# Sums of the down weights made inside the block products, and gate products placed behind later copies

## The chip, the cores and the metric

The kernel runs on one core of a Trainium2 chip. The metric is the time of one execution in microseconds on the device, and lower is better. A run is an execution of the whole kernel, and the times given are medians over runs.

## The reference

The reference is a two-layer encoder over 768 tokens, a sample of 512 and a prompt of 256, each going through the layers by itself, with a model width of 1024. Layer 0 mixes tokens with a bidirectional mLSTM, layer 1 with sliding-window attention. Both are followed by a feed-forward net with a gate and a convolution of width 3 along the tokens. All is float32.

```python
for l in range(DEPTH):                      # 2
    ...
    y = mlstm_mixer(...) if l == 0 else swa_mixer(...)   # both end in "@ w_out"
    x = x + g1 * y
    h = rmsnorm(x, norm_g[l, 1]) * (1 + sc2) + sh2
    x = x + g2 * conv_ffn(h, ffn_w_up[l], ffn_conv_w[l], ffn_conv_b[l], ffn_w_down[l])
return rmsnorm(x, final_g)

def conv_ffn(h, w_up, conv_w, conv_b, w_down):
    u = h @ w_up                            # 768 x 1024 @ 1024 x 5632
    u = depthwise_conv3(u, conv_w) + conv_b
    g, val = u[..., :2816], u[..., 2816:]
    return (silu(g) * val) @ w_down         # 768 x 2816 @ 2816 x 1024
```

The change concerns the feed-forward net, above all its down projection, and what runs during the projection (`out_proj`) that ends the mixer before it.

## The kernel before, in words

**Precision.** Every float32 operand of a matmul is split into a high and a low part: ScalarE (ACT) casts the high one (L263), VectorE (DVE) subtracts it for the low one (L264), and TensorE (PE) makes three matmuls, high by high, high by low, low by high. A weight tile of 128x1024 float32 (512 KB) arrives by DMA in one of five `raw` buffers and is split into one of three `whi` and one of three `wlo` buffers.

**Up projection and gate.** The 2816 columns of the gate are 22 chunks of 128, taken two at a time as 11 parts (`up(p)`). A part needs two `pair` calls, one for the gate columns and one for the values. A pair is computed by a Strassen-Winograd scheme: seven block products, called quarters here, of 12 matmuls each, with the names B11, T1, T2, B21, T3, B22, T4. The sums of weights that this needs are made by POOL (GpSimd) from two loaded weight tiles (L1206, L1209, L1210, L1218); `wa`, `wb` and `wc` are the split weights. Sums of results are formed in PSUM: a "fork copy" on ACT copies a running sum from one bank to another (L1221 ahead of T2, L1234 after it), so that the quarter after it can add on top. Evictions (L1247, L1248 on DVE, L1186 and others on ACT) put the results in a row buffer. Then comes the convolution: ACT does the middle tap (L1484), DVE the outer two (L1486, L1487), and ACT the SiLU (L1494). 

**Gate product and operands.** Parts 2 to 9, eight parts, go through the blocked down projection. For such a part `operands` lets POOL multiply gate and values (L1511, four instructions) and DVE form the sums that the blocked scheme needs as right-hand operands (L1514 to L1517). The seven operands of a part are stored to DRAM (`yd`, L1521, issued by SP a pair later). Part 9's stay on the chip (`final`). Parts 0, 1 and 10 are multiplied by `product` (L1499) and projected directly by `down`.

**Blocked down projection.** `blocked` multiplies the down weights of the eight parts, as 2x2 blocks over their output columns and the parts' two chunks, with the operands in seven products of 96 matmuls each (Strassen-Winograd once more, 8 steps of k a product). A product's weights are four tiles of 512 KB, one for two steps of k. It accumulates in four X or four Y banks in PSUM; ACT copies banks to banks and DVE adds them to x (L593). Loads of weights are at L1303, loads of operands from `yd` at L1298; L383 loads x again, which had been saved to `xf`.

**Sums.** Four of the seven products need sums of the given weight blocks. `sums(l)` makes them ahead of time: it loads the 16 weight tiles of the eight parts, makes the sums on POOL (L1262, L1264, L1266, L1269; 32 instructions of 128x512 a layer) and stores them to DRAM as `sd` (16 stores). It is a generator, stepped three times after each tile of `out_proj` through `self.fills`. In layer 1 it also runs beside attention.

**Order.** A scheduler orders the instructions of each engine by its estimate of readiness and by program order. `issue_after` ties instructions behind a named one, and `manual_schedule` keeps the written order on the engines it lists. SP issues the loads and stores in the order of its queue and waits in it for buffers to come free.

Of the kernel before, what the change touches and what calls it, by code (L numbers as in the profile page):

```python
# [169 lines left out]
class Net:  # L170
    def __init__(self, tc, ctx, io):
        self.tc, self.nc, self.io = tc, tc.nc, io
        pool = lambda n, **k: ctx.enter_context(tc.tile_pool(name=n, bufs=1, **k))
        self.cp = pool("consts")
        self.hp = pool("acts")
        self.stg = pool("stage")
        self.big = pool("big")
        self.nt = pool("normtmp")
        self.psp = pool("psum", space=bass.MemoryType.PSUM)
        self.dp = pool("scratch", space=bass.MemoryType.DRAM)  # L180
        self.turn = 0
        self.n = 0
        self.fill = iter(())
        self.pend = []

        self.early, self.begun = {}, {}
        self.sd = {}
# [407 lines left out]
    def out_proj(self, u0, act, xt, l, apply):  # L595
# [26 lines left out]
        for i, (z, c, w) in enumerate(todo):  # L622
            if i in (KC, 2 * KC - 1):
                yield
            c0, c1, _ = HALVES[z]
            o = self.ps()[:, : c1 - c0]
            self.product(o, w, act, c0, c1, range(self.begun.pop(i, 0), KC))
            self.tick(4.2)
            for p0, p1, q in pieces(c0, c1):
                self.resid(xt, o[:, p0 - c0 : p1 - c0], l, 16, c, (p0, p1, q))  # L630
            norms[z].square(c)
            self.step(self.fills, 3)
            if i % KC == KC - 1:
                self.start(HALVES[z], norms[z].stages())
# [617 lines left out]
    def sums(self, l):  # L1252

        nc = self.nc
        tt = nc.gpsimd.tensor_tensor
        self.sd[l] = sd = self.dp.tile([NBLK, P, 2048], F32, name=f"sd{l}")
        for k in range(NBLK):
            u = U_FFN + (l * NPART + SOLO + k) * 3 + 2
            r = [self.load(u, h) for h in range(2)]
            s2, s4, s1, s3 = (t[:, 512 * i : 512 * (i + 1)] for t in r for i in range(2))  # L1260
            yield
            tt(s1, s1, s3, ALU.add)  # L1262
            yield
            tt(s2, s1, s2, ALU.subtract)  # L1264
            yield
            tt(s4, s4, s2, ALU.subtract)  # L1266
            nc.sync.dma_start(sd[k, :, :1024], r[0])
            yield
            tt(s3, s3, s2, ALU.subtract)  # L1269
            nc.sync.dma_start(sd[k, :, 1024:], r[1])  # L1270
            yield

    def blocked(self, l, xt, u, yd, xf):
# [3 lines left out]
        w, sd = self.io["w"], self.sd[l]  # L1277

        def given(i):
            return lambda k: w[u + 3 * k : u + 3 * k + 4 : 3, :, 512 * i : 512 * (i + 1)]  # L1280

        def summed(i):
            return lambda k: sd[k : k + 2, :, 512 * i : 512 * (i + 1)]
# [5 lines left out]
        parts = {}  # L1289

        def ready(i):
            if i >= len(stream):
                return
            src, z = stream[i]
            ys = self.slab([P, NBLK - 1, H])
            for k in K[::4]:
                e = min(k + 4, NBLK - 1)
                nc.sync.dma_start(ys[:, k:e], yd[k:e, :, z].rearrange("k p t -> p k t"))  # L1298
            ys = [ys[:, k] for k in K[:-1]] + [self.final[:, z]]
            for k in K:  # L1300
                if k % 2 == 0:
                    raw = self.stg.tile([P, 2, 512], F32, tag="raw", name=self.nm("raw"), bufs=5)
                    nc.sync.dma_start(raw, src(k).rearrange("k p c -> p k c"))  # L1303
                    wt = self.split(raw.rearrange("p k c -> p (k c)"))
                y = [self.tmp([P, H], R) for _ in range(2)]
                self.fp_copy_split(*y, ys[k])
                parts[i, k] = [t[:, 512 * (k % 2) : 512 * (k % 2 + 1)] for t in wt], y

        X = [self.pa()[:, :H] for _ in range(4)]
        Y = [self.bank[c][:, :H] for c in range(4)]  # L1310

        def add(c, c0, o):
# [6 lines left out]
            (X, late, True, lambda c: nc.scalar.copy(Y[c], X[c])),  # L1319
            (X, soon, False, lambda c: add(c, 0, X[c])),  # L1320
            (Y, late, False, lambda c: nc.scalar.copy(X[c], Y[c])),
            (Y, soon, False, lambda c: add(c, H, Y[c])),
            (X, late, False, lambda c: add(c + 4, H, X[c])),
            (Y, late, True, lambda c: (add(c, H, Y[c]), add(c + 4, H, Y[c]))),
            (X, late, False, lambda c: add(c + 4, 0, X[c])),
# [142 lines left out]
    def ffn(self, l, xt, pool, last_tile, apply, keep=None):  # L1468
# [10 lines left out]
        stores = []  # L1479
# [16 lines left out]
        def product(yrow, g):  # L1496
            for j in range(2):
                y = yrow[:, 2 + j]
                nc.gpsimd.tensor_tensor(y, y, yrow[:, j], ALU.mult)  # L1499
                self.fp_copy_split(g[:, 0, j], g[:, 1, j], y)  # L1500

        yd = self.dp.tile([NBLK - 1, P, 7, H], F32, name=f"yd{l}")

        def operands(yrow, k):
# [7 lines left out]
            b11, t3, b21, b22, t2, t4, t1 = (s[:, z] for z in range(7))  # L1512
            tt = nc.vector.tensor_tensor
            tt(t3, b22, t3, ALU.subtract)  # L1514
            tt(t2, b11, t3, ALU.add)
            tt(t4, b21, t2, ALU.subtract)
            tt(t1, b22, t2, ALU.subtract)  # L1517
            if k == NBLK - 1:
                self.final = s
                return  # L1520
            return lambda: nc.sync.dma_start(yd[k], s)  # L1521

        def up(p):
# [9 lines left out]
            for i in range(2):  # L1533
                if p:
                    rows = [urow[:, 2 * i + j] for j in range(2)]
                    with ExitStack() as order:
                        then = [held.pop()] if held else []
# [3 lines left out]
                        if i and stores:  # L1541
                            then.append(stores.pop())
# [5 lines left out]
                if i == 0:  # L1548
                    held.append(lambda: silu(yrow))
            if g is None:  # L1550
# [51 lines left out]

        prev = None
        for p in range(NPART):
            g = up(p)
            if prev is not None:
                down(*prev)
            if p == SOLO:
                xf = self.dp.tile([P, KC, T], F32, name=f"xf{l}")
# [3 lines left out]
        self.blocked(l, xt, u0 + 3 * SOLO + 2, yd, xf)  # L1613
# [20 lines left out]
    def block(self, l, act, xs):  # L1634

        with self.tc.tile_pool(name="ffn", bufs=1, reuse_waits="tile") as pool:
# [3 lines left out]
            self.fills = self.sums(l)  # L1640
# [156 lines left out]
```

## Time and profile before

| | |
|---|---|
| median of 3 runs | 1905.57 us (1902.56 to 1913.9) |
| profiled execution, its own time | 1909.98 us |
| its span, first to last instruction | 1908.2 us |
| mean granted TensorE clock | 0.970 |
| PE busy | 1793.6 us, 94% |
| DVE busy | 1378.4 us, 72% |
| ACT busy | 955.4 us, 50% |
| POOL busy | 602.6 us, 32% |
| moved by the main DMA queue | 279.90 MB |

Times in the table are microseconds. A share is busy time over the span and is an average over stages that have different limits. The bracket behind a row, such as `[1.55 <-ACT ps L1221]`, is how long the engine was idle just before that instruction and whose result ended the wait. A granted clock of 1.00 is full speed of TensorE.

### The profile page before, as it was taken

The page shows a single profiled execution, that of the slowest core. Times are in us where ns is not written, and L with a number is a line of the kernel's source. Part 1 is how long each engine was busy: PE and PEld are TensorE (multiplying, and loading weights), DVE is VectorE, ACT ScalarE, POOL GpSimd, SP SyncE. Part 2 cuts the span into 40 slices and gives each one's busy share as a digit, 9 for nine tenths or more (in the row PEclk, how much of TensorE's full clock was granted, in tenths as well). Part 3 has the DMA queues.
Part 4 walks back from the last instruction along what each step waited for, and adds up shares of the span by engine and source line. Part 5 has one row for each costly group of instructions (what it writes and reads, how often), then busy time and mean ns, then how long its engine had stood idle before and what let it go on. Part 6 is the DMA issues. An engine that isn't in the chain of part 4 may idle for free.

```text
span 1908.2 us, 29324 instructions
## 1 busy us (share of the span) xinstructions
PE 1793.6 (94%) x11098; PEld 1679.8 (88%) x11098; DVE 1378.4 (72%) x2077; ACT 955.4 (50%) x1935; POOL 602.6 (32%) x482
## 2 busy tenths in 40 slices
PE   6999999998799999999799999999999999997997
PEld 4988887988798999999799989889989989997997
DVE  4765677884589877787666767756898777877665
ACT  3444443442356445555454556654564455554543
POOL 2101001025514544655200203645134455542001
PEclk7999999999899999999899999999999999998999
DMA  8343566457822243232665321457222432336652
GB/s 323 114 157 120 177 211 214 153 172 245 296 72 79 89 140 125 95 124 97 220 202 178 123 78 51 153 165 262 81 79 77 150 125 96 114 105 193 218 168 67
DMA packets 111769, 281.77 MB, mean 148 GB/s; under 512 B 8631, under 2 KB 51127, under 8 KB 109836
## 3 DMA queue, kind: packets, MB, share of 16 engines
q1 hardware_dynamic: 111628, 279.90, 44.1%
q8 instruction: 87, 1.43, 0.3%
q14 instruction: 54, 0.44, 0.1%
HBM read 231.09 MB, written 48.77 MB: 147 GB/s over the span
## 4 chain that ended last, share of the span: by engine, by line
PE 44%; DVE 13%; POOL 5%; issue 5%; ACT 5%; DMA 4%; POOLq 0%; SPq 0%; DVEq 0%; ACTq 0%
PE pa L257 7%; PE ps L257 6%; PE ps L1173 6%; PE ps L1176 5%; PE ps L1174 5%; DMA raw<-in_w_dram 3%; DVE wlo L264 3%; PE pa L1338 2%; PE pa L1339 2%; PE pa L1337 2%; PE ps L1338 2%; PE ps L1337 2%; PE ps L1339 2%; ACT whi L263 2%; DVE slab L1486 2%
## 5 line engine op out<-in xcount | busy, mean ns | idle before, releaser
L264 DVE TENSOR_TENSOR wlo<-raw,whi 128x1024 fp32r<-128x1024 f32 x261 | 351.6, 1348 | 126.5 <-ACT whi L263 120.5
L263 ACT CAST whi<-raw 128x1024 fp32r<-128x1024 f32 x261 | 272.9, 1047 | 200.9 <-DMA raw<-in_w_dram 65.3
L1173 PE MATMUL ps<-zh,whi 128*128 128x384 f32 x504 | 172.7, 343 | 22.4 <-ACT ps L1221 22.0
L257 PE MATMUL ps<-zh,whi 128*128 128x256 f32 (+1 forms) x560 | 189.6, 340 | 2.5 <-ACT whi L263 1.9
L257 PE MATMUL ps<-zh,wlo 128*128 128x256 f32 (+1 forms) x560 | 185.1, 332 | 2.0 <-DVE wlo L264 2.0
L257 PE MATMUL ps<-zl,whi 128*128 128x256 f32 (+1 forms) x560 | 185.5, 333 | 0.0
L1176 PE MATMUL ps<-zh,wlo 128*128 128x384 f32 x504 | 171.7, 341 | 0.5 <-DVE wlo L264 0.4
L1174 PE MATMUL ps<-zl,whi 128*128 128x384 f32 x504 | 171.3, 340 | 0.8 <-DVE zl L1130 0.8
L257 PE MATMUL ps<-slab,whi 128*128 128x384 f32 x512 | 137.8, 351 | 14.6 <-ACT whi L263 14.1
L1484 ACT ACTIVATE slab<-slab,cstt 128x772 f32<-128x772 f32 x88 | 91.0, 1034 | 113.2 <-DVE slab L1247 112.2
L1486 DVE SCALAR_TENSOR_TENSOR slab<-slab,cstt,slab 128x771 f32<-128x771 f32 x88 | 114.7, 1305 | 35.4 <-ACT slab L1484 35.3
L257 PEld LDWEIGHTS ps<-zh,whi 128*128 128x128 f32 x560 | 107.8, 193 | 16.1 <-issue 4.4
L1173 PEld LDWEIGHTS ps<-zh,whi 128*128 128x128 f32 x504 | 95.6, 190 | 29.0 <-ACT ps L1221 26.8
L509 DVE SCALAR_TENSOR_TENSOR ada<-raw,silc,ada 128x1024 f32<-128x1024 f32 x84 | 110.2, 1349 | 14.8 <-DMA raw<-in_adaln_w_dram 14.8
L1206 POOL TENSOR_TENSOR raw<-raw 128x512 f32<-128x512 f32 x40 | 63.1, 1579 | 180.2 <-DMA raw<-in_w_dram 168.1
L1511 POOL TENSOR_TENSOR slab<-slab 128x512 f32<-128x512 f32 x64 | 97.5, 1544 | 66.7 <-DVE slab L1487 54.7
L257 PEld LDWEIGHTS ps<-zh,wlo 128*128 128x128 f32 x560 | 107.5, 192 | 12.4 <-DVE wlo L264 2.9
L257 PEld LDWEIGHTS ps<-zl,whi 128*128 128x128 f32 x560 | 107.6, 193 | 12.1 <-issue 3.4
L257 PEld LDWEIGHTS ps<-slab,whi 128*128 128x128 f32 x512 | 95.1, 195 | 18.6 <-ACT whi L263 17.3
L263 ACT CAST nt<-slab 128x384 fp32r<-128x384 f32 x112 | 56.8, 512 | 108.8 <-PE pa L1338 61.9
L1176 PE MATMUL ps<-yh,wlo 128*128 128x384 f32 x304 | 105.5, 347 | 4.7 <-DVE wlo L264 4.5
L264 DVE TENSOR_TENSOR nt<-slab,nt 128x384 fp32r<-128x384 f32 x112 | 60.7, 553 | 67.8 <-ACT nt L263 67.8
(316 smaller groups left out, 5175.9 us busy)
## 6 DMA issues: line engine op xcount, KB each, us to landing
raw<-in_w_dram SPq DMA_DIRECT2D x232, 512.0 KB, 4.1
raw<-in_adaln_w_dram SPq DMA_DIRECT2D x84, 512.0 KB, 4.5
yd<-slab SPq DMA_DIRECT2D x14, 1344.0 KB, 4.6
sd<-raw SPq DMA_DIRECT2D x32, 512.0 KB, 4.1
raw<-sd SPq DMA_DIRECT2D x32, 512.0 KB, 4.2
slab<-yd SPq DMA_DIRECT2D x14, 768.0 KB, 7.1
slab<-yd SPq DMA_DIRECT2D x14, 576.0 KB, 8.3
slab<-in_x_dram SPq DMA_DIRECT2D x12, 512.0 KB, 7.5
```

Of the source, the lines that this page charges most:

```text
L257: self.nc.tensor.matmul(out, lhsT, rhs, start=start, stop=stop)
L263: nc.scalar.copy(hi, src)
L264: return nc.vector.tensor_tensor(lo, src, hi.bitcast(F32), ALU.subtract)
L509: stt(acc[:, s], row, w, acc[:, s], ALU.mult, ALU.add)
L1173: mm(o, wh[:, k], hi[k], start=start and k == 0, stop=False, skip_group_check=True)
L1174: mm(o, wh[:, k], lo[k], start=False, stop=False, skip_group_check=True)
L1176: mm(o, wl[:, k], hi[k], start=False, stop=k == 3, skip_group_check=True)
L1337: mm(o[c], wh[:, cs], yh, start=start and k == 0, stop=False, skip_group_check=True)
L1338: mm(o[c], wh[:, cs], yl, start=False, stop=False, skip_group_check=True)
L1484: nc.scalar.activation(y, u, AF.Identity, bias=cb, scale=w(1))
L1486: stt(y[:, 1:], u[:, :-1], w(0), y[:, 1:], ALU.mult, ALU.add)
L1511: nc.gpsimd.tensor_tensor(row[:, p0:p1], yrow[:, 2 + j, b], yrow[:, j, b], ALU.mult)
```

## The change

The DRAM pass is gone: `sums`, `self.fills` and `self.sd` are removed. `blocked` makes the sums when it needs them. Its seven products come in a new order, with S1T1 (operand 6, weights a21 + a22) first. The columns of `stream` are the operand's index z, the two weight blocks, the engine and operation of the sum, and the index under which the sum is kept in DRAM for a later product. Kept sums are stored from POOL's own DMA queue.

```diff
-        stream = [
-            (given(0), 0), (given(1), 2), (summed(0), 4), (summed(1), 3), (summed(3), 1), (summed(2), 6), (given(3), 5),
-        ]
+        stream = [
+            (6, a21, a22, gp, ALU.add, 0),
+            (0, a11, None, None, None, None),
+            (2, a12, None, None, None, None),
+            (4, saved(0), a11, gp, ALU.subtract, 1),
+            (1, a11, a21, tt, ALU.subtract, None),
+            (3, a12, saved(1), tt, ALU.subtract, None),
+            (5, a22, None, None, None, None),
+        ]
...
+            z, a, b, op, how, keep = stream[i]
             for k in K:
                 if k % 2 == 0:
-                    raw = self.stg.tile([P, 2, 512], F32, tag="raw", name=self.nm("raw"), bufs=5)
-                    nc.sync.dma_start(raw, src(k).rearrange("k p c -> p k c"))
-                    wt = self.split(raw.rearrange("p k c -> p (k c)"))
+                    r = raw(a(k))
+                    if b:
+                        op(r, r, raw(b(k)), how)
+                    if keep is not None:
+                        nc.gpsimd.dma_start(sd[keep][k // 2], r)
+                    wt = self.split(r)
```

Per layer the weights of the products take 44 loads of 512 KB in place of 28, and 8 stores; the pass with its 16 loads and 16 stores falls away. The sums are 8 POOL and 8 DVE instructions of 128x1024 in place of 32 POOL instructions of 128x512. The results go to banks and to x in an order that fits (the first product is added to two rows of x at once, so the reload of x is needed by its end):

```diff
-            (X, late, True, lambda c: nc.scalar.copy(Y[c], X[c])),
-            (X, soon, False, lambda c: add(c, 0, X[c])),
...
+            (X, late, True, lambda c: (add(c, H, X[c]), add(c + 4, H, X[c]))),
+            (Y, late, True, lambda c: nc.scalar.copy(X[c], Y[c])),
+            (Y, soon, False, lambda c: add(c, 0, Y[c])),
+            (X, late, False, lambda c: nc.scalar.copy(Y[c], X[c])),
+            (Y, soon, False, lambda c: add(c + 4, H, Y[c])),
+            (X, late, False, lambda c: add(c, H, X[c])),
+            (Y, late, False, lambda c: add(c + 4, 0, Y[c])),
```

Second, `operands` is called behind a fork copy of the next part's second pair, and its DVE combinations behind one of the pair after that; the store follows them. `yd` becomes three DRAM tiles, of the first 4, the next 2 and the last part.

```diff
-            return lambda: nc.sync.dma_start(yd[k], s)
+            def combine():
+                b11, t3, b21, b22, t2, t4, t1 = (s[:, z] for z in range(7))
+                tt = nc.vector.tensor_tensor
+                tt(t3, b22, t3, ALU.subtract)
+                tt(t2, b11, t3, ALU.add)
+                tt(t1, b22, t2, ALU.subtract)
+                tt(t4, b21, t2, ALU.subtract)
+                if k < NBLK - 1:
+                    nc.sync.dma_start(yd[k // 2 - 1][k % 2] if k > 3 else yd[0][k], s)
+                else:
+                    self.final = s
+            later[SOLO + k + 2, 0] = combine
...
             if g is None:
-                stores.extend(filter(None, [operands(yrow, p - SOLO)]))
+                later[p + 1, 1] = lambda: operands(yrow, p - SOLO)
```

Third, `blocked` becomes a generator (`tail`) that asks for the operands of the first two products earlier, six parts of them at the start of part 10 and the seventh after its first pair; later products' operands are asked for two products ahead in place of one.

```diff
+        fetch(0, (0, 1))
+        fetch(1, (0, 1))
+        yield
+        fetch(0, (2,))
+        fetch(1, (2,))
+        yield
...
+        ready(0)
+        xt[:] = self.load_x(xf)
         for i, (o, order, start, done) in enumerate(steps):
-            for j in (0, 1) if i == 0 else (i + 1,):
-                ready(j)
-            if i == 0:
-                xt[:] = self.load_x(xf)
+            ready(i + 1)
+            fetch(i + 2)
```

In the changed file the lines shift: POOL's sums in `pair` are L1204, L1207, L1208, L1216, the fork copies L1219 and L1232, the weight loads L1289, the sums in `blocked` L1300, their stores L1302, the products L1510, the combinations L1515 to L1518, the block matmuls L1342 to L1344.

More of the change, by code (lines that the diff above doesn't have):

```diff
@@ L1250, in pair @@
         self.evict(r2, d)
[L1252 to L1271, printed above, removed]
@@ L1478, in ffn @@
         behind = []
-        stores = []
+        later = {}
         def conv(u, y, ch):
@@ L1536, in up @@
                     with ExitStack() as order:
[L1537 removed]
+                        then = [f for f in (held.pop() if held else None, later.pop((p, i), None)) if f]
                         for ins in behind[2 * i :] if p == 1 else ():
                             order.enter_context(self.tc.issue_after(ins))
[L1541 to L1542 removed]
                         other = p == i == 1
```

74 lines of the change are left out of this document (37 added, 37 removed).

## The prediction

> **What bounds the kernel now.** I read the page first, then TensorE's idle time in order of place, then the windows around each place.
>
> ```profile
> core 0: 1908.2 us, clock 0.970
> PE 1793.6 (94%) x11098; PEld 1679.8 (88%) x11098; DVE 1378.4 (72%) x2077; ACT 955.4 (50%) x1935; POOL 602.6 (32%) x482
> L1173 PE MATMUL ps<-zh,whi 128*128 128x384 f32 x504 | 172.7, 343 | 22.4 <-ACT ps L1221 22.0
> ```
>
> TensorE is the bound: busy for 1793.6 of 1908.2 us, so 114.6 us are idle. The change leaves the matmuls as they are. It can only win idle time back, and the little that TensorE loses by a lower clock after an idle stretch. The third row names one lump already: 22.0 us in which the first matmul of a quarter waits for the fork copy L1221. I take the four places that the change touches one by one. In the windows below the columns are stretch, length, busy time (and count) of PE, PEld, DVE, ACT, POOL, then granted clock, DMA share, GB/s.
>
> **1. The sums leave layer 0's output projection.** Removed, per layer, are 16 loads and 16 stores of 512 KB and 32 POOL adds of 128x512 that ran during `out_proj`.
>
> ```profile
> 440.00:460.00 20.00, 16.30 (x88) 15.16 (x87) 11.84 (x14) 5.34 (x9) 12.95 (x9) 0.94 0.92 317
> 460.00:480.00 20.00, 18.40 (x101) 17.76 (x101) 11.21 (x13) 4.52 (x6) 13.88 (x9) 0.98 0.78 280
> 480.00:500.00 20.00, 17.73 (x106) 17.00 (x104) 8.54 (x13) 6.50 (x9) 7.91 (x7) 0.96 0.93 316
> 500.00:520.00 20.00, 13.55 (x56) 11.76 (x56) 9.69 (x21) 7.01 (x15) 15.04 (x11) 0.78 0.82 287
> 520.00:540.00 20.00, 18.30 (x103) 18.30 (x103) 18.09 (x27) 12.66 (x26) 1.80 (x3) 0.91 0.56 186
> ```
>
> And what waits for what in 430 to 545, with its transfers:
>
> ```profile
> ACT whi L263 <- DMA raw<-in_w_dram: 28.3, 7, 9.4
> SPq L272 <- DMA sd<-raw: 21.4, 12, 4.1
> DMA packets 8844, 28.03 MB, mean 244 GB/s; under 512 B 864, under 2 KB 2400, under 8 KB 8837
> ```
>
> The five windows add up to 84.3 busy us of 100: 15.7 idle. The slow stretch costs more: 56 matmuls in 13.55 us are 0.242 each, against 18.30/103 = 0.178 in the next window, 56 x 0.064 = 3.6 us. The last three rows say what is late: the copy that starts a weight split waits 28.3 us for weights, and SP, which issues every load, is held 21.4 us by buffers still being stored to `sd`. Of the 28.03 MB, 32 transfers of 0.524 MB, 16.8 MB, are the sums'. Without them 11.2 MB are left for the same stretch and SP's queue holds loads alone. At most 15.7 + 3.6 = 19.3 us come back, about 21 if the edges of the stretch gain too; I keep two for the first weights and the norm at its end: **-17** (-10 to -21; the low end is half of the idle time and the slow matmuls).
>
> **2. The same in layer 1**, where the sums also ran beside attention.
>
> ```profile
> sum 150.00, PE 143.12 PEld 133.88 DVE 104.86 ACT 81.98 POOL 74.28; mean PE 47.71 PEld 44.63 DVE 34.95 ACT 27.33 POOL 24.76
> ```
>
> The wait itself:
>
> ```profile
> PE pa L1012 <- POOL t L1004: 2.2, 1, 2.2
> ```
>
> From 1210 to 1360 PE is idle for 6.9 us only; one wait of 2.2 is for a POOL step of attention that stands behind the adds. **-4** (-2, that wait alone, to -7, all of it).
>
> **3. Combinations behind the copies in the up projection.** The four POOL products (L1511) move behind the fork copy of the next part's second pair; the four DVE combinations (L1514 to L1517) get a place of their own after them; the `yd` store follows at once. Windows of six consecutive parts:
>
> ```profile
> 723.90:756.10 32.20, 30.66 (x176) 30.30 (x175) 25.06 (x24) 18.86 (x32) 17.14 (x12) 1.00 0.30 107
> 756.10:787.90 31.80, 29.82 (x170) 29.35 (x168) 25.36 (x25) 16.89 (x30) 18.89 (x12) 1.00 0.32 110
> 787.90:821.10 33.20, 31.59 (x170) 30.95 (x170) 25.61 (x25) 19.05 (x32) 17.75 (x12) 0.95 0.31 105
> 821.10:852.80 31.70, 29.72 (x170) 29.25 (x168) 25.26 (x25) 16.80 (x30) 18.68 (x12) 1.00 0.31 109
> 852.80:886.10 33.30, 31.69 (x170) 31.05 (x170) 25.71 (x25) 19.19 (x32) 17.57 (x12) 0.95 0.32 107
> 886.10:916.10 30.00, 29.61 (x169) 29.28 (x168) 24.90 (x25) 16.67 (x30) 14.41 (x10) 1.00 0.24 71
> ```
>
> The chain of one stall:
>
> ```profile
> 874.89 1.07 DVE L1514 TENSOR_TENSOR slab<-slab 128x384 f32<-128x384 f32 x1 [1.20 <-POOL slab L1511]
> 880.18 0.55 DVE L1247 TENSOR_TENSOR slab<-ps,nt 128x384 f32<-128x384 f32 x1
> 880.81 1.04 ACT L1484 ACTIVATE slab<-slab,cstt 128x772 f32<-128x772 f32 x1 [5.07 <-DVE slab L1247]
> 885.02 0.47 ACT L1221 COPY ps<-ps 128x384 f32<-128x384 f32 x1
> 885.54 0.44 PE L1173 MATMUL ps<-zh,whi 128*128 128x384 f32 x1 [1.55 <-ACT ps L1221]
> ```
>
> The chain reads: DVE waits for POOL's products (874.89), combines, evicts L1247 only at 880.18; ACT had waited 5.07 us for that with the first tap of the convolution and gets to the fork copy at 885.02; PE waits 1.55. In two parts the clock falls to 0.95 as well. The first five parts take 162.2/5 = 32.44 us, the one without a stall 30.0: 2.4 us for each of five parts in two layers are 24.4 at most, the 22.0 idle of the first fence and some clock. In the new instruction order DVE's evictions stand ahead of the combinations and ACT's fork copy ahead of the second convolution, which takes this chain away. But the combinations now wait on DVE for POOL in the pair's middle, and behind them stand the low parts of wb and of the next pair's wa. I put the pair together from the durations above: the next wa is ready at 14.8 us of the pair and needed at 15.05. That is no slack, so some pairs stall for a fraction: **-17** (-8 to -24).
>
> **4. The start of the block products.** Before, the first product's operands come late:
>
> ```profile
> 920.00:930.00 10.00, 6.44 (x37) 6.12 (x35) 7.26 (x11) 7.10 (x11) 0.33 (x1) 0.93 0.49 157
> 930.00:940.00 10.00, 2.64 (x7) 2.24 (x8) 6.72 (x8) 3.32 (x6) 4.70 (x2) 0.50 0.96 324
> 940.00:950.00 10.00, 10.00 (x54) 10.00 (x53) 3.67 (x6) 3.96 (x6) 0.00 (x0) 0.89 1.07 358
> ```
>
> What ends that wait:
>
> ```profile
> 929.06 2.66 SPq L1298 DMA_DIRECT2D slab<-yd  x4
> 933.10 2.57 POOL L1499 TENSOR_TENSOR slab<-slab 128x772 f32<-128x772 f32 x1 [0.96 <-ACT slab L263]
> 937.00 0.69 PE L1337 MATMUL pa<-nt,whi 128*128 128x384 f32 x1 [10.56 <-ACT nt L263]
> 1752.87 0.69 PE L1337 MATMUL pa<-nt,whi 128*128 128x384 f32 x1 [10.64 <-ACT nt L263]
> ```
>
> The y loads are issued only at 929.06, and ACT's first y copy stands behind a copy that waits for POOL's product of part 10 (933.10). PE stands for 10.6 us in either layer, and after it runs slowly: 7 matmuls in 2.64 us at clock 0.50 and 54 instead of 59 in the next window, 1.5 + 0.8 = 2.3 us. Up to 13 us per layer.
>
> After, the y operands are asked for at the start of part 10 and the first weights behind pair (10,0). What is late next is on POOL. Its order in the built program is: weight sums of pair (10,0), first block sum L1300, store L1302, second L1300, then the sums of pair (10,1), between them the four products of part 9, then the last sum of that pair. The second L1300 needs a load that waits for a `raw` buffer which the first frees.
>
> ```profile
> 915.67 0.45 PE L1173 MATMUL ps<-zh,whi 128*128 128x384 f32 x1 [0.40 <-ACT ps L1221]
> L1511 POOL TENSOR_TENSOR slab<-slab 128x512 f32<-128x512 f32 x64 | 97.5, 1544 | 66.7 <-DVE slab L1487 54.7
> raw<-in_w_dram SPq DMA_DIRECT2D x232, 512.0 KB, 4.1
> L1269 POOL TENSOR_TENSOR raw<-raw,raw 128x512 f32<-128x512 f32 x8 | 12.6, 1571 | 0.0
> ```
>
> A sum of 128x1024 is twice the 128x512 one: 3.1 us (1571 ns). From the second L1300's load to the last pair's `wc` lie 4.1 + 3.1 + four products 6.2 = 13 us, of which POOL had some 6 idle there before. So T2 of the last pair, which began at 915.67, starts some 7 us later (bounds 2, when the loads come early, and 13). Of 13 us I credit 13 - 7 = 6, less 1 for the casts still ahead: 5 per layer, **-10** (0 to -22).
>
> **5. Inside the block products.** Added per layer are 16 loads, 8 stores (from POOL's queue), 8 POOL and 8 DVE operations of 128x1024.
>
> ```profile
> DMA packets 14936, 25.57 MB, mean 206 GB/s; under 512 B 727, under 2 KB 8794, under 8 KB 14925
> 1760.00:1770.00 10.00, 10.00 (x59) 10.00 (x58) 5.41 (x8) 5.64 (x9) 0.00 (x0) 1.00 1.06 359
> L264 DVE TENSOR_TENSOR wlo<-raw,whi 128x1024 fp32r<-128x1024 f32 x28 | 34.3, 1224 | 10.8 <-ACT whi L263 10.8
> L264 DVE TENSOR_TENSOR nt<-slab,nt 128x384 fp32r<-128x384 f32 x55 | 29.9, 553 | 33.9 <-ACT nt L263 33.9
> slab<-yd SPq DMA_DIRECT2D x14, 576.0 KB, 8.3
> ```
>
> The first row is the stretch 938 to 1062, layer 0's products. 59 matmuls in 10 us make 16.3 us a product of 96, 4.1 per pair of k. Bytes: 25.57 + 24 x 0.524 = 38.2 MB in 124 us, 308 GB/s, below the 359 that one window moved with PE full. DVE in the products with a difference needs 4 x (1.22 + 1.22 + 2 x 0.55) = 14.2 us of 16.3, plus adds to x. POOL's 3.1 us fit in 4.1. Five `raw` buffers: the sum's own is held for load 4.1, add 3.1, store 4.1 (a plain load's), the other for 4.1 + 3.1; 18.5/5 = 3.7 us per pair of k, below 4.1. With loads and stores at the 8.3 of the last row it is 31.1/5 = 6.2, 2.1 too slow over 8 pairs of k: 17 us per layer. Three split weights in hand give 12 us against it. I take near the first: **+4** for both layers (0 to +24).
>
> The Trainium skill, "SBUF — State Buffer", section "SBUF: two separate sides", has a rule against this place: a VectorE operation with both inputs in SBUF and a GpSimd operation that reads SBUF exclude each other for the whole instruction. If POOL's 3.1 and DVE's 1.22 + 1.10 took turns, a pair of k would need 5.4 us where 4.1 are to be had, 5 us per product in two products and, beyond the weights in hand, nothing to 20 us in all. The sum by the overlap is +4, by the full exclusion up to +20. The rows show adds at 1571 ns beside other work, no more than that.
>
> **Sum.** -17 - 4 - 17 - 10 + 4 = -44 on the profiled execution's 1909.98 (span 1908.2, 1.8 around it): **1866 us**. That execution is 4.4 above the median of 1905.57, so 1862 would be as well founded; I stay with its own time.
>
> **Rivals.**
> - *Block products partly starved.* The 17 us per layer of term 5, less the weights in hand, leave some 12: +24 in place of +4 gives 1886, and with a little less from the start 1890. For it: stores through a queue that this trace never used. Against: half of the stretch moved under 206 GB/s with PE full.
> - *The fork stalls only move.* If DVE, waiting for POOL in the pair, delays T3 or the next B11 by as much as L1221 was delayed, term 3 is 0: 1883. For it: no slack at 14.8 of 15.05.
> - *Out_proj stays slow*, since its idle time was its own weights' latency: terms 1 and 2 give nothing: 1887. Against: 92% DMA share there.
> - *Slower than before: the transfers and sums that cost out_proj 16 us cost the block products more.* In `out_proj` they went at 244 GB/s on average. At that rate the 38.2 MB take 157 us, 33 more than 124 per layer: -48 + 65 = +17, 1927. It decides from 38.2 MB in 124 + 24 us, 258 GB/s, downward. Against: 317, 280 and 316 GB/s in three windows of that same stretch.
>
> **How the numbers follow.** Forecast 0.54; starved 0.15; stalls move 0.13; out_proj stays 0.07; slower 0.11. Faster by over 1% (below 1886.5, about what a measurement here can tell from no change) holds the forecast and the moved stalls, 0.67, and 0.02 of the starved case, whose better half ends there: 0.69. Within 1%: the rest of the starved case and the out_proj case, 0.13 + 0.07 = 0.20. Slower 0.11. The range goes from all terms near their best, 1846, to 1898, where the starved case has ended; what is left out is mostly the slower case.
>
> **What would show it.** Right: windows of 440 to 540 with PE at 19 or more of 20 and DMA share under 0.5; the group of L1219 (the fork copy then) without its 22 us; parts of 30 to 31 us; a start gap under 3 us, and a new wait of 5 to 9 us in the last pair's T2 for the low part of `wc`; PE full in the products, at over 270 GB/s. Wrong: PE waiting for weights inside products 4, 1 or 3, POOL's stores taking over 8 us, or T3 and B11 waiting for DVE in every part.

## The result and the profile after

The changed kernel takes 1889.38 us (median of 4 runs, 1882.77 to 1893.23) against 1907.47 before (1902.56 to 1913.9): a ratio of 0.990, 95% interval 0.9856 to 0.9943. That is 18 us where 44 was forecast. The profiled execution spans 1891.4 us where that of before spanned 1908.2.

The page of the kernel after, with its first lines, the two lines of TensorE's largest waits, and the DMA issues that are new or longer:

```profile
PE 1791.8 (95%) x11098; PEld 1674.2 (89%) x11098; DVE 1365.6 (72%) x2093; ACT 952.3 (50%) x1935; POOL 553.0 (29%) x450
...
L1171 PE MATMUL ps<-zh,whi 128*128 128x384 f32 x504 | 175.6, 348 | 22.3 <-ACT whi L262 13.6
L1174 PE MATMUL ps<-zh,wlo 128*128 128x384 f32 x504 | 175.9, 349 | 21.2 <-DVE wlo L263 21.2
...
raw<-in_w_dram SPq DMA_DIRECT2D x248, 512.0 KB, 4.2
sd<-raw POOLq DMA_DIRECT2D x16, 512.0 KB, 5.6
raw<-sd SPq DMA_DIRECT2D x16, 512.0 KB, 5.6
```

The first matmul of a quarter is idle for 22.3 us as before (22.4), and the third, which takes the low part of the weight, has 21.2 us of its own that it did not have. By span less busy time, TensorE's idle time fell by 15 us in all, from 114.6 to 99.6. Where the time went is read from places that both traces have: the fork copies ahead of T2 (L1221 before, L1219 after), and the first and last matmul of the block products. Times are starts in us, and the last column is what each stretch gave or took.

| place | before | after | after - before | stretch |
|---|---|---|---|---|
| first fork copy, layer 0 (end of out_proj) | 577.46 | 551.15 | -26.3 | -26.3 |
| fork copy in part 9's second pair, layer 0 | 885.02 | 858.53 | -26.5 | -0.2 |
| first matmul of the block products | 937.0 | 916.2 | -20.8 | +5.7 |
| end of the block products | 1056.5 | 1038.8 | -17.7 | +3.1 |
| first fork copy, layer 1 (after its mixer) | 1393.19 | 1365.85 | -27.3 | -9.6 |
| fork copy in part 9's second pair, layer 1 | 1700.77 | 1672.27 | -28.5 | -1.2 |
| first matmul of the block products | 1752.9 | 1728.4 | -24.4 | +4.1 |
| end of the block products | 1872.3 | 1851.1 | -21.2 | +3.2 |
| end of the span | 1908.2 | 1891.4 | -16.8 | +4.4 |

The two stretches with the removed pass gave 36 us, not 21. The up projection gave 1.4 in place of 17. The start of the block products took 10 where it should have given 10, and inside them it took 6. The last +4.4 belongs to this one execution: TensorE went at a clock of 0.53 for 10 us (1867 to 1877) in the final projection, and none of the other traces has it (their last stretch is 36 to 37 us, as before's 35.9). So most of the 4.4 says nothing about the change.

The windows of `out_proj` from 440 on, 20 us each as in the prediction and with its columns. The stage begins at the same time in both kernels and ends 26 us earlier here, so the fourth window holds its end:

```profile
440.00:460.00 20.00, 20.00 (x118) 20.00 (x117) 14.30 (x21) 10.51 (x15) 0.86 (x1) 1.00 0.78 265
460.00:480.00 20.00, 20.00 (x122) 20.00 (x120) 8.51 (x16) 5.35 (x9) 0.00 (x0) 1.00 0.38 119
480.00:500.00 20.00, 20.00 (x119) 20.00 (x120) 15.63 (x33) 14.30 (x34) 0.85 (x1) 1.00 0.30 92
500.00:520.00 20.00, 19.59 (x121) 19.27 (x120) 16.95 (x24) 7.39 (x14) 6.38 (x6) 1.00 0.23 71
```

TensorE is full and its clock 1.00. 118 to 122 matmuls go into 20 us; before it was 56 to 106 at clocks of 0.78 to 0.98. The first three windows need 60 us for 359 matmuls, 0.167 us each; at that rate the 454 matmuls of the prediction's five windows would have taken 76 of their 84.3 busy us. So the slow clock took some 8 us there, an estimate from these rows. The prediction priced it in one window only, at 3.6.

Part 3's second pair and the last pair of layer 0, from the timelines of POOL, ACT, DVE and PE of the kernel after:

```profile
657.94 4.66 POOL L1510 TENSOR_TENSOR slab<-slab 128x512 f32<-128x512 f32 x4
662.57 1.60 POOL L1208 TENSOR_TENSOR raw<-raw 128x512 f32<-128x512 f32 x1
670.25 0.69 PE L1174 MATMUL ps<-zh,wlo 128*128 128x384 f32 x1 [4.33 <-DVE wlo L263]
...
881.67 2.39 POOL L1300 TENSOR_TENSOR raw<-raw,raw 128x1024 f32<-128x1024 f32 x1 [6.40 <-DMA raw<-in_w_dram]
888.49 3.08 POOL L1300 TENSOR_TENSOR raw<-raw,raw 128x1024 f32<-128x1024 f32 x1 [3.33 <-DMA raw<-in_w_dram]
891.54 2.00 POOL L1207 TENSOR_TENSOR raw<-raw,raw 128x512 f32<-128x512 f32 x1
894.10 3.84 POOL L1510 TENSOR_TENSOR slab<-slab 128x512 f32<-128x512 f32 x4
897.90 1.25 POOL L1208 TENSOR_TENSOR raw<-raw 128x512 f32<-128x512 f32 x1
899.18 1.04 ACT L262 CAST whi<-raw 128x1024 fp32r<-128x1024 f32 x1 [7.10 <-POOL raw L1208]
900.28 0.69 PE L1171 MATMUL ps<-zh,whi 128*128 128x384 f32 x1 [6.60 <-ACT whi L262]
903.98 0.69 PE L1174 MATMUL ps<-zh,wlo 128*128 128x384 f32 x1 [2.69 <-DVE wlo L263]
```

In both places POOL makes the gate products (L1510) ahead of the pair's own weight sum (L1208). The cast of `wc` waits for that sum, and T2 waits for the cast. In the last pair the second block sum (L1300) has first held POOL until its load came. L1207, L1510 and L1208 stand behind it on POOL and wait with it. The waits are followed by a slow clock:

```profile
670.00:675.00 5.00, 4.75 (x15) 4.75 (x16) 2.47 (x3) 1.14 (x3) 2.38 (x2) 0.50 0.72 253
900.00:905.00 5.00, 2.03 (x5) 1.52 (x6) 4.97 (x7) 2.56 (x5) 0.37 (x1) 0.50 0.00 0
905.00:910.00 5.00, 4.45 (x14) 3.94 (x14) 1.66 (x2) 1.96 (x3) 2.29 (x1) 0.50 0.76 232
910.00:915.00 5.00, 5.00 (x26) 5.00 (x25) 2.30 (x2) 2.62 (x5) 3.06 (x3) 0.82 0.83 282
```

At clock 0.50 a matmul is issued every 0.32 us and not every 0.17. So the waits of 9.8 us in the last pair cost some 15: 26.4 us pass from its fork copy (889.73) to the first block matmul, and before it was 11.3 from the fork copy to the end of the pair (915.13 to 926.44).

A later part (part 7's second pair and the pair after it) shows the new small stall, on DVE and PE:

```profile
797.93 1.08 DVE L1515 TENSOR_TENSOR slab<-slab 128x384 f32<-128x384 f32 x1 [1.90 <-POOL slab L1510]
798.93 1.21 DVE L263 TENSOR_TENSOR wlo<-raw,whi 128x1024 fp32r<-128x1024 f32 x1
800.20 0.45 PE L1174 MATMUL ps<-zh,wlo 128*128 128x384 f32 x1 [0.42 <-DVE wlo L263]
805.21 0.45 PE L1174 MATMUL ps<-yh,wlo 128*128 128x384 f32 x1 [0.52 <-DVE wlo L263]
```

The combination L1515 heads DVE's queue and waits for POOL. The low part of a weight whose high part is ready stands behind it. The two PE rows are the quarters T3 and the next pair's B11.

### The profile page after: what moved, and what is told of

The parts are those of the page before. It is cut to its first block, busy times and chain, and to the rows that moved or that the text cites. A ratio compares the mean times of both kernels' runs of the same rounds, so it can differ in the third digit from the quotient of the medians.

```text
span 1891.4 us, 29178 instructions
## 1 busy us (share of the span) xinstructions
PE 1791.8 (95%) x11098; PEld 1674.2 (89%) x11098; DVE 1365.6 (72%) x2093; ACT 952.3 (50%) x1935; POOL 553.0 (29%) x450
## 4 chain that ended last, share of the span: by engine, by line
PE 55%; DVE 13%; POOL 12%; DMA 9%; issue 7%; ACT 3%; SPq 0%; POOLq 0%; DVEq 0%; ACTq 0%
PE ps L256 24%; PE pa L256 10%; DMA raw<-in_w_dram 7%; POOL slab L1510 4%; DVE wlo L263 4%; PE ps L1174 3%; PE ps L1171 3%; PE ps L1172 3%; POOL raw L1208 2%; PE ps L1343 2%; PE ps L1342 2%; PE ps L1344 2%; POOL raw L1207 2%; POOL raw L1204 2%; PE pa L1010 1%
## 5 line engine op out<-in xcount | busy, mean ns | idle before, releaser
L263 DVE TENSOR_TENSOR wlo<-raw,whi 128x1024 fp32r<-128x1024 f32 x261 | 339.4, 1303 | 103.3 <-ACT whi L262 102.5
L1171 PE MATMUL ps<-zh,whi 128*128 128x384 f32 x504 | 175.6, 348 | 22.3 <-ACT whi L262 13.6
L1174 PE MATMUL ps<-zh,wlo 128*128 128x384 f32 x504 | 175.9, 349 | 21.2 <-DVE wlo L263 21.2
L1204 POOL TENSOR_TENSOR raw<-raw 128x512 f32<-128x512 f32 x40 | 64.9, 1623 | 270.2 <-DMA raw<-in_w_dram 246.9
L256 PE MATMUL ps<-slab,whi 128*128 128x384 f32 x512 | 132.3, 340 | 0.9 <-DVE slab L263 0.5
L1491 DVE SCALAR_TENSOR_TENSOR slab<-slab,cstt,slab 128x771 f32<-128x771 f32 x88 | 105.2, 1197 | 36.9 <-ACT slab L1489 36.8
L1174 PEld LDWEIGHTS ps<-zh,wlo 128*128 128x128 f32 x504 | 97.8, 194 | 28.2 <-DVE wlo L263 26.6
L256 PEld LDWEIGHTS ps<-zh,wlo 128*128 128x128 f32 x560 | 107.5, 192 | 11.7 <-DVE wlo L263 2.4
L1492 DVE SCALAR_TENSOR_TENSOR slab<-slab,cstt,slab 128x771 f32<-128x771 f32 x88 | 113.8, 1293 | 0.3
L1171 PE MATMUL ps<-yh,whi 128*128 128x384 f32 x304 | 103.7, 341 | 0.0
L1172 PE MATMUL ps<-yl,whi 128*128 128x384 f32 x304 | 103.5, 341 | 0.0
```

Source lines behind the costliest of these rows:

```text
L256: self.nc.tensor.matmul(out, lhsT, rhs, start=start, stop=stop)
L263: return nc.vector.tensor_tensor(lo, src, hi.bitcast(F32), ALU.subtract)
L1171: mm(o, wh[:, k], hi[k], start=start and k == 0, stop=False, skip_group_check=True)
L1172: mm(o, wh[:, k], lo[k], start=False, stop=False, skip_group_check=True)
L1174: mm(o, wl[:, k], hi[k], start=False, stop=k == 3, skip_group_check=True)
L1204: tt(q[2], q[2], q[3], ALU.add)
```

## The experiments

Each was timed in three rounds beside the kernel before. The medians of before in the four sets were 1909.7, 1908.0, 1908.3 and 1906.8; ratios are to the before of the same set. The befores of the sets differ by 3 us, and the kernel after was timed in a fifth set (before 1907.47), so a difference of 2 or 3 us between medians of different sets says nothing.

**The pass alone.** The kernel before without `sums`:

```diff
-            self.step(self.fills, 3)
...
-            self.fills = self.sums(l)
...
-            (given(0), 0), (given(1), 2), (summed(0), 4), (summed(1), 3), (summed(3), 1), (summed(2), 6), (given(3), 5),
+            (given(0), 0), (given(1), 2), (given(0), 4), (given(1), 3), (given(3), 1), (given(2), 6), (given(3), 5),
```

> The kernel before without its pass over the down weights during out_proj and attention (no loads, no POOL adds, no stores to sd); four of the seven block products take plain weight blocks where they took stored sums, so their loads stay as many but the result is another. The trace of after reaches the end of out_proj 26 us earlier than before in layer 0 and gains 10 us more in the mixer of layer 1. Theory A (the pass itself cost all of that, idle time and the lower clock after it): 36 us below before, about 1871. Theory B (the prediction's sizes, 17 + 4): about 1886. Theory C (that time was the projection's own weights): no change.

1872.55 us, ratio 0.9796 (0.9774 to 0.9819). The first fork copies are at 552.0 and 1356.3: 25.5 us earlier than before in layer 0 and 11.4 more in layer 1 (10.1 of them from the end of layer 0's block products on), and the rest of the trace runs as before. Theory A: the pass cost 37 us. The change kept only half of what its first part brings.

**The placement alone.** The kernel before with `combine`, `later[p + 1, 1]` and `later[SOLO + k + 2, 0]` as in after:

> The kernel before with the products and combinations placed as after, and nothing else of the change. Prediction's term 3: 17 us below before, about 1892. Theory A (waits only move; a stall of 5 to 7 us in part 3's second pair and one for wc in the last pair take what the fork copies give): between 5 below and 10 above before, 1904 to 1919.

1909.96 us (10 runs), ratio 1.0016 (0.9999 to 1.0032). Its waits of PE, kernel with the placement alone:

```profile
PE pa L1337 <- ACT nt L263: 22.8, 2, 11.9
PE ps L1176 <- DVE wlo L264: 21.9, 24, 4.3
...
PE ps L1173 <- ACT ps L1221: 5.8, 12, 1.7
```

Of the 22 us for fork copies 5.8 are left, and 21.9 us for low parts stand beside them (4.9 before), in 24 places, the longest 4.3 in part 3's second pair. As built, the placement is worth nothing. The rival "the fork stalls only move" is what happened.

**The placement undone in the changed kernel.** After, with `operands` called as before, right behind its part:

```diff
-                later[p + 1, 1] = lambda: operands(yrow, p - SOLO)
+                operands(yrow, p - SOLO)
```

> The kernel after with the gate products and combinations of parts 2 to 9 placed as before (right behind a part's second pair; store a pair later), all else as after. Theory A (the new place only moves the stalls: 22 us of waits for fork copies come back, but the waits for low parts and the stall of some 7 us in part 3's second pair go, and POOL has four products less in the last pair): 5 to 15 us below after, 1875 to 1885. Theory B (the new place is worth the predicted 17 us): about 1906.

1872.76 us, ratio 0.9793 (0.9765 to 0.982), 17 us below after; lower than either theory had it. Here the new placement costs 17 us, where it cost nothing in the kernel before. In this kernel POOL's four products of part 9 meet the block sums in the last pair: from the fork copy in part 9's second pair to the first block matmul it is 47.1 us in layer 0 and 43.9 in layer 1 with the old placement, and 57.6 and 56.2 in after. Inside the products 3 and 5 us of that are lost again.

**POOL's order mended.** Two kernels of after, the second with both edits:

```diff
-        tt(q[2], q[3], q[0], ALU.subtract)
+        own = tt(q[2], q[3], q[0], ALU.subtract)
...
-            with self.tc.issue_after(fork.ins):
+            with self.tc.issue_after(fork.ins), self.tc.issue_after(own.ins):
                 behind()
```

> The kernel after with one tie added: the products called behind a pair stand on POOL behind that pair's own last weight sum. It moves POOL's order at two places per layer, part 3's second pair and the last pair. Theory A (wc made late by the products costs 6 to 7 us at the first place and half of the 15 us at the second): 20 to 28 us below after, 1861 to 1869. Theory B (PE waits there for transfers in any order): no change.

1881.52 us, ratio 0.9838 (0.9815 to 0.9861), about 8 below after where 20 to 28 were expected. The first place is mended: part 4's second fork copy is 3.5 us earlier than in after, though this trace was 1.8 us later at the first fork copy. In the last pair only a part is won (51.7 us from part 9's fork copy to the first block matmul in place of 57.6), since L1300 still stands ahead of L1207.

```diff
-                        op(r, r, raw(b(k)), how)
+                        with self.tc.issue_after(self.hold.ins) if i == 0 else ExitStack():
+                            op(r, r, raw(b(k)), how)
```

Here `self.hold` is the last of part 9's POOL products.

> As the kernel with the products behind the pair's own sums, and also the sums of the first block product stand on POOL behind part 9's products, so nothing of the block products is ahead of the last pair's weight sums. Theory A (the first two block sums, one of them waiting for its load, hold up the last pair): the whole 15 us per layer come back, about 1850 to 1858. Theory B (the first product's weights then come too late and the old start gap opens instead): no better than the kernel with the products alone moved, 1865 or more.

1872.48 us, ratio 0.9793 (0.9759 to 0.9827): 17 below after and 9 below the first edit alone, less than the 31 to 39 of theory A. T2 of the last pair in layer 0 no longer waits, and the first block matmul of layer 0 comes at 900.0, in after at 916.2. But a later quarter of the pair now waits 2.65 us for an ACT copy, with a slow clock behind it, so that 18.1 us pass from the pair's fork copy to the first block matmul, and the block products take 126.9 us in layer 0 in place of 122.6. Order on POOL accounts for about as much as undoing the placement does.

**The combinations behind wb.** The kernel above, and what a pair calls behind its second fork copy, the DVE combinations among it, tied behind the low part of `wb`:

> As the kernel with the products and the first sums moved back on POOL, and the DVE combinations stand behind the low part of wb of the pair that they are called in. Theory A (PE's 20 us of waits for low parts, 0.5 to 1.6 us each at 28 places, come from combinations that stand ahead of a weight's low part while they wait for POOL): most of these waits go, 12 to 20 us below that kernel's 1872, about 1852 to 1860. Theory B (DVE is full in these pairs in any order, 25 of 32 us busy, and the waits move to evictions and fork copies): 1872 within 4.

1864.13 us, ratio 0.9768 (0.9745 to 0.9791), 8 lower by the medians and between the two theories. The intervals of the two kernels overlap, so the gain of the whole isn't clear of noise; where it comes from is seen in the trace. The waits for low parts of weights leave the list of PE's largest; 14.7 us for ACT L1184 and 9.0 for an ACT copy come in. The up projection from part 3's second pair to part 9's takes 189.1 us in layer 0 in place of 194.5 without this tie and 199.3 before, but the block products 132.0 in layer 0.

**Early y operands.** The kernel with the old placement, and `fetch(0)`, `fetch(1)` moved behind both `yield`s:

> The kernel with the products placed as before, but the y operands of the first two products are asked for only when these are made, as before the change. Theory A (asking early took the start gap away): the gap of 10 us comes back in each layer, 1885 to 1895. Theory B (the gap was from ACT's casts behind part 10's product, and goes because the first weights are ready early): 1873 within 4.

1898.73 us, ratio 0.9947 (0.9926 to 0.9969): 26 us above that kernel, more than expected. The gap of before is back, as the second row of this kernel's timeline shows; the first is the last pair's wait for its fork copy, which grew too (2.47 with the early request):

```profile
891.98 0.69 PE L1171 MATMUL ps<-yh,whi 128*128 128x384 f32 x1 [5.06 <-ACT ps L1219]
918.05 0.69 PE L1340 MATMUL pa<-nt,whi 128*128 128x384 f32 x1 [11.76 <-ACT nt L262]
```

So asking early takes the gap away, and as built it is the one edit beside the removed pass that brings time.

**What the sums inside cost.** Four kernels, all with the old placement. First, plain weight blocks only:

> The kernel with the products placed as before, and the block products take plain weight blocks: no second load, no sum on POOL or DVE, no store (the sums are left out, the result is another). Steps and operands as in after. Theory A (transfers and sums inside the block products cost 6 to 8 us per layer): the seven products go from 125 and 128 us to 119 or 120, 12 to 16 us below that kernel's 1873, about 1859. Theory B (the new order of steps, with a wait of 2 us for ACT's copies, and DVE's crowd at the start cost it): 3 to 5 us below at most.

1847.62 us, ratio 0.968 (0.9662 to 0.9698): 25 us below the kernel with the sums, so that is what they cost, at the start of the block products (6 and 3 us in the traces of the two layers) and inside (7 and 10). It is also 25 us below the kernel before without its pass (1872.55), which has the late y operands and the old order of products: asking early is worth as much without the sums as with them. Second, the same with the second blocks loaded but not used:

> The kernel with the products placed as before; second blocks are loaded into the buffers as in after, but neither added nor stored (sums left out, the result is another). Against the kernel with plain blocks (1848) it has 16 loads more per layer. Theory A (the engines' sums and what waits for them cost the 25 us): 1848 within 4. Theory B (transfers cost it): 1860 or more.

1847.99 us, ratio 0.9686 (0.9667 to 0.9704): the loads cost nothing when no sum holds their buffers. Third, sums without their stores (two products take plain blocks where they took stored sums):

> The kernel with the products placed as before; the sums in the block products stay, but nothing is stored for a later product: the two products that take a stored sum load a plain block there (so those sums are others, and the result too). Loads and adds as many as before. Theory A (stores, and loads that wait for them, hold the buffers): 8 to 15 us below 1873. Theory B (loads and adds cost it): 1873 within 4.

1872.01 us, ratio 0.981 (0.9792 to 0.9827), the same as with them: the stores cost nothing either. Fourth, all sums on DVE:

> The kernel with the products placed as before, and all sums in the block products on DVE (the 8 of POOL per layer too). In the trace of that kernel's like, DVE's weight lows last 3.2 to 3.4 us in place of 1.2 beside POOL's 128x1024 adds. Theory A (POOL's sums, and DVE shut out beside them, cost a large part of the 25 us): 8 to 15 us below that kernel's 1873, about 1861. Theory B (DVE is the crowded one, and 2 x 4 more operations of 1.2 us per layer make it worse): 1873 to 1880.

1870.75 us, ratio 0.9803 (0.9782 to 0.9824): nearly no gain, so theory A falls, and the loss of theory B didn't come either. The windows of the block products of layer 0, first with loads only, then with sums on POOL and DVE and the old placement:

```profile
897.00:1015.00 118.00, 117.05 (x673) 116.15 (x672) 82.18 (x117) 60.73 (x95) 4.11 (x2) 1.00 0.82 273
904.80:1030.30 125.50, 120.93 (x675) 119.50 (x674) 98.90 (x126) 59.72 (x95) 19.73 (x12) 0.97 0.83 283
```

273 GB/s are moved with TensorE full and 283 with TensorE late: not the transfers. What differs is that sums wait, and what waits behind them. Of the kernel with all sums on DVE, in the last pair:

```profile
899.17 1.23 DVE L1300 TENSOR_TENSOR raw<-raw,raw 128x1024 f32<-128x1024 f32 x1 [4.55 <-DMA raw<-in_w_dram]
900.31 1.02 DVE L1492 SCALAR_TENSOR_TENSOR slab<-slab,cstt,slab 128x771 f32<-128x771 f32 x1
901.42 0.85 ACT L1499 ACTIVATE slab<-slab 128x772 f32<-128x772 f32 x1 [3.86 <-DVE slab L1492]
```

A sum stands at the head of DVE's queue for 4.55 us until its load lands. The convolution of the last pair is behind it, and ACT behind that.

**The place of the first sums.** The kernel with all sums on DVE and the old placement, with the first product's sums tied behind the last pair's low part of `wb`:

```diff
-                        op(r, r, raw(b(k)), how)
+                        with self.tc.issue_after(self.wb.ins) if i == 0 else ExitStack():
+                            op(r, r, raw(b(k)), how)
```

> The kernel with the products placed as before and all block sums on DVE (1871), with one tie more: the first product's sums stand on DVE behind the last pair's low part of wb. It tells whether the 25 us that sums cost are a matter of order at the start of the block products or of the sums' own time. Theory A (order: a sum that waits for its load at the head of DVE's queue holds up the last pair): 1855 to 1862. Theory B (the time of the sums, spread over the products): 1871 within 4.

1862.73 us, ratio 0.9761 (0.9741 to 0.9781): 8 of the 25 us are the place of the first sums. The last pair is as with plain blocks (11.1 us from fork copy to first block matmul in both), but inside the products 8.7 and 10.6 us more (in the traces) than with plain blocks remain. Neither theory alone holds. Counted off by 96 matmuls, a product runs at 16.6 us when nothing holds it. Here the first takes 19.4 us in layer 0 (20.3 in layer 1) where the loads alone give 16.9 (16.6), and the fifth and sixth, whose sums stand on DVE in every kernel with sums, 18.8 and 20.5 (19.0 and 20.4) in place of 16.6. In the sixth PE waits 1.97 us for the low part of a weight.

**The best of it.** The kernel with POOL's order and the combinations mended, with all sums on DVE and the first ones behind `wb`:

> The kernel with the combinations behind the low part of wb, and all sums of the block products on DVE, those of the first product behind the last pair's wb. If POOL's sums cost the block products time, 1850 to 1858, against 1864 with the sums on POOL; if DVE has no room there, 1864 to 1872.

1849.11 us, ratio 0.9689 (0.967 to 0.9708): 40 below after and 59 below before. That is the time of the kernel without the sums and with the old placement (1847.62), but the sums have not become free. The products still take 124.9 us in either layer, where that kernel has 118.1 and 117.7; the up projection from part 3's second pair to part 9's pays for it, with 189.1 and 190.0 us in place of 197.7 and 198.9.

Beside the kernel of the paragraph before (1862.73) this one has the new placement with its order mended, and nothing else: 13.6 us less, with intervals that don't touch. So the place behind the fork copy does pay, once the operations that wait stand behind the weight sum and the low part of `wb`.

Beside the kernel of "The combinations behind wb" (1864.13) its sums are on DVE and not behind POOL's products: 15 us less. In the traces 6.5 of them per layer lie between the last pair's fork copy and the first block matmul (18.7 and 12.2 us). First POOL, DVE, ACT and PE of that kernel there, then DVE here:

```profile
885.18 5.75 POOL L1302 TENSOR_TENSOR raw<-raw,raw 128x1024 f32<-128x1024 f32 x2
888.64 2.72 DVE L1518 TENSOR_TENSOR slab<-slab 128x384 f32<-128x384 f32 x1
892.38 0.85 ACT L1501 ACTIVATE slab<-slab 128x772 f32<-128x772 f32 x1 [3.40 <-DVE slab L1494]
894.09 0.69 PE L1171 MATMUL ps<-zh,whi 128*128 128x384 f32 x1 [4.48 <-ACT nt L1244]
...
887.84 0.55 DVE L1518 TENSOR_TENSOR slab<-slab 128x384 f32<-128x384 f32 x1
```

A combination that takes 0.55 us here took 2.72 beside two POOL sums. DVE's convolution came late behind it, ACT's copy behind that, and PE stood 4.48 us.

## Why the prediction was right or wrong, point by point

- *Terms 1 and 2, the pass (-21).* Right in mechanism, mis-sized: 37 us. The step that failed is the sizing of the slow clock. It was counted in one window, 3.6 us, though clocks of 0.91 to 0.98 stood in the others, where some 8 us in all were lost. In layer 1, -4 was taken from the idle time of 150 us alone (6.9 us), while the pass cost some 10 there. With the pass gone TensorE fills whole windows of 20 us in layer 0: the idle time kept back for "the first weights" was not needed. The rival that `out_proj` stays slow falls with it.
- *Term 3, the combinations (-17).* Wrong for the change as built: nothing by itself. The chain to L1221 was read rightly and did go. What failed is the value taken for the new place, "some pairs stall for a fraction": the prediction's own durations left a slack of 0.25 us, and a place without slack was priced near the good end. The place itself is worth 13.6 us (1862.73 to 1849.11), close to the forecast, when nothing that waits for POOL stands ahead of a weight's low part. The stall at part 3's second pair, 4.33 us and a slow clock behind it, was in the built order, which puts L1510 ahead of L1208 at that pair, and was read only for the last one.
- *Term 4, the start (-10).* The mechanism named for what is late next, POOL's order in the last pair, is what the trace shows. It was sized at 7 us and measured at 15, since two waits of 6.60 and 2.69 put the clock at 0.50 for 10 us. The gain from the early y operands was sized right: 26 us over both layers with the sums, where the removed gaps and their slow clock are up to 13 per layer. The stretch took 10 us instead of giving 10. The wait that was named, 5 to 9 us in the last pair's T2, did come, as 6.60 for the high part and 2.69 for the low part of `wc`.
- *Term 5, inside (+4).* Wrong in size and in reason. The sums cost 25 us over the start and the inside. The bandwidth, on which the bounds rested with the buffers, costs nothing (1847.99 with all loads, 1872.01 without the stores). What the buffers cost that a waiting sum holds isn't shown: no kernel has the sums and more buffers. What was left out is that a sum adds a wait between a load and a cast on two engines that work in order.
- *The sum.* -44 was predicted and -18 measured. The 18 is what two opposite errors left: the pass was worth 16 us more than forecast, the other three terms together some 40 less. By the experiments, -37 for the pass, -26 for early y, +25 for the sums, and +17 for the placement on top of them add to -21; the other 3 are within the spread of the runs.
- *Rivals.* "The fork stalls only move" held for the change as built, with T3 and B11 waiting as it said. "Partly starved" gave about the right time (1886 to 1890) by luck: its transfers cost nothing, and 17 less 12 us leave 5 per layer and not the 12 that it counted. The slower case didn't come: the products took 3 us more per layer and not 33, at 281 and 262 GB/s.
- *The Trainium skill*, "SBUF — State Buffer", section "SBUF: two separate sides", was weighed against term 5. The trace agrees that the two engines exclude each other: beside POOL's L1300 of 881.67 to 884.06 a DVE low part of 1.2 us lasts 3.17. With all sums on DVE and the old placement the time stayed (1870.75), so there the exclusion is not what the sums cost. With POOL's order mended, the 2.72 us for a combination of 0.55 beside POOL's sums are of the same kind, and the kernel with these sums on DVE is faster; no run tells this apart from the sums' place in POOL's queue.

```profile
881.97 3.17 DVE L263 TENSOR_TENSOR wlo<-raw,whi 128x1024 fp32r<-128x1024 f32 x1 [1.09 <-ACT whi L262]
```

Open: what makes weights late inside the products, which costs some 7 us per layer even in the best kernel. It may be DVE's own time (busy for 101.6 of 125.0 us there) or the buffers that waiting sums hold.

## What to carry to other kernels

Waits that stand at the head of an engine's queue are paid by whatever stands behind them, so the price of a moved step is read from the built order at every place where it occurs, the first and the last repetition above all, and not from a typical one. Work for the next stage belongs behind the last weight sum of this stage, on each engine in question, but no further back: behind POOL's products the first sums came late again. An idle stretch of TensorE is to be priced with the slow clock after it, as those of 2.65, 4.33 and 9.8 us here.

## What the runs showed of the hardware that was not expected

A short stall costs more than its length: the 9.8 us of waits in the last pair cost 15. After 4.33 us of wait, 15 matmuls went out in 5 us at clock 0.50; after 6.60 and 2.69 us, 19 in 10 us, the second wait included, where 59 in 10 us is the full rate. The Trainium skill, "TensorE: Matmul & The Clock Gate", section "Part 1: The HAM clock gate", has the clock halved after an idle window of about 3.4 us; the trace agrees for these two. A shorter wait was enough elsewhere: with POOL's first sums moved back, PE waited 2.65 us (to 896.33), and the clock from 897 to 899 was 0.50, with matmuls 0.32 us apart. The clock also fell to 0.53 for 10 us in the final projection of the profiled execution of after, behind waits of 0.45 and 0.62 us only; the trace doesn't say why.
